# Gate and up projections as a 2x2 block product with seven products, the down projection in two passes, and weights split 1024 columns at a time

## The chip, the core and the metric

One Trainium2 chip, one of its cores. The metric is the device time of one execution in microseconds (us); lower is better. A core has a matrix engine (TensorE, in the profile PE, its weight loads PEld), a vector engine (VectorE, DVE), a scalar engine (ScalarE, ACT), a general engine (GpSimd, POOL) and queues that start transfers (SyncE, SP). Each engine takes its instructions in the order of its own list and waits for the others by semaphores.

## The reference

One transformer block on 512 tokens of width 1024 in float32: a norm, four token mixers (a forgetting attention, a short convolution, a chunkwise mLSTM, a sliding-window attention) with gated outputs, a merge product, and then the feed-forward part, which is where the change lies:

```python
h = rms_norm(x, ffn_norm[l])
act = jax.nn.silu(jnp.einsum('bsd,df->bsf', h, w_gate[l])) * jnp.einsum('bsd,df->bsf', h, w_up[l])
x = x + jnp.einsum('bsf,fd->bsd', act, w_down[l])      # D = 1024, D_FF = 2816 = 22 x 128
```

## The kernel before

Everything is held transposed: features on the 128 partitions, the 512 tokens along a row. A product of a 128 x 128 block of weights with 512 tokens is one matmul with the weights stationary. Precision comes from splitting: each float32 operand becomes a high part `hi` (a cast on ACT) and a remainder `lo` (`src - hi` on DVE), in `split` (L132); `mm3` (L127) then issues three matmuls, hi x hi, hi x lo and lo x hi, so every block product costs three.

All weights stream from one array of tiles of 1024 columns (512 KB). `w_load` (L151) starts a transfer on SP, `w_split` (L160) splits half a tile, 512 columns, into a pair of tiles from a ring of nine, and `w_take` (L174) hands out pairs some ahead of their use. `proj` (L394) makes one 128 x 512 output: eight input blocks, 24 matmuls.

The part around the change, in its order:

- Merge: eight outputs `mg` (L797). DVE adds the residual (`x`, L799), ACT and DVE scale and split it into `x2h`, `x2l` (L802), ACT squares it, and POOL adds the squares into `ssq` (L809) for the norm.
- 22 units, one for each 128 columns of the hidden layer (L814): `fg` (gate) and `fu` (up), 24 matmuls each, 48 in a unit. DVE multiplies both from PSUM by the norm's factor `r` (L820, L822), ACT applies Silu, POOL multiplies the two (L823), and the result is split into `ah`, `al`.
- Down: eight outputs `dn` (L831), each over all 22 units, 66 matmuls; DVE adds the residual and SP writes the block out.

Pools of fixed depth set when a buffer comes free: `wraw` for raw weight tiles, `whi`/`wlo` for split ones, eight PSUM banks in two pools (`mm`, `at`) of four. The program's instructions are put in order by a scheduler that works on a model of the times; the order that it gave is shown below where it matters.

## Time and profile before

| | us |
|---|---|
| Three runs | 863.06, 863.35, 864.82; median 863.35 |
| The profiled execution's own time | 862.88 |
| Its span in the trace | 861.1 |
| Mean granted clock of TensorE | 0.994 of full speed |
| Merge products, first to last start | 454.2 to 497.5 |
| Gate and up products, first to last start | 497.8 to 737.4 |
| Down products, first to last start | 737.6 to 857.1 |

The span is divided among stages that follow one another on PE. A busy PE is read with care, because matmuls overlap and their ends are modelled: the distance between the starts of two neighbours is what one costs. DVE, ACT and POOL rows have a real duration each; where a duration differs from the usual one for its shape, the instruction was held up while it ran. The idle time of an engine and its releaser say whom it waited for.

### The profile page before, as it was taken

How to read it: one execution, taken by the hardware profiler on the slowest of the kernel's cores; microseconds unless marked ns; L12 is line 12 of the kernel's file. 1: busy time of each engine (PE TensorE's matmuls, PEld its weight loads, DVE VectorE, ACT ScalarE, POOL GpSimd, SP SyncE). 2: the span in 40 equal slices, each digit the busy share in tenths (PEclk: the TensorE clock that was granted, in tenths of full speed). 3: DMA queues.
4: the chain of work that ended last, by engine and by line, in shares of the span. 5: the costliest groups of instructions: out<-in, count | busy, mean ns of one | idle time of the engine just before them, and what ended most of it. 6: DMA issues, size and time to landing. Idle time of an engine off the chain costs nothing.

```text
span 861.1 us, 10668 instructions
## 1 busy us (share of the span) xinstructions
PE 846.6 (98%) x3879; PEld 699.6 (81%) x3879; DVE 493.4 (57%) x899; ACT 386.1 (45%) x733; POOL 144.9 (17%) x134
## 2 busy tenths in 40 slices
PE   7999999999999999999999999999999999999998
PEld 6877788888788888888888888888888888888886
DVE  6899966459888886675745545444444333522320
ACT  7565555467665654554534444333333322322210
POOL 5262100024312001221211202111111111000000
PEclk9998999999999999999999999999999999999999
DMA  6642222242221522222224423222222232233310
GB/s 232 214 136 97 87 74 74 96 125 73 74 74 50 172 83 88 75 74 98 98 98 141 150 78 120 94 99 89 97 94 96 97 99 97 97 123 110 123 37 24
DMA packets 28520, 87.35 MB, mean 101 GB/s; under 512 B 3455, under 2 KB 5032, under 8 KB 28468
## 3 DMA queue, kind: packets, MB, share of 16 engines
q1 hardware_dynamic: 24716, 80.87, 27.6%
q10 hardware_dynamic: 3752, 5.81, 2.3%
q8 instruction: 30, 0.49, 0.2%
...
## 4 chain that ended last, share of the span: by engine, by line
PE 84%; DVE 8%; ACT 3%; issue 2%; DMA 2%; SPq 0%; POOL 0%; DVEq 0%; ACTq 0%; POOLq 0%
PE dn L130 5%; PE fu L128 5%; PE dn L129 5%; PE fg L128 5%; PE fu L130 5%; PE fg L130 5%; PE fu L129 5%; PE fg L129 5%; PE dn L128 5%; PE gswa L129 2%; PE gswa L128 2%; PE gswa L130 2%; PE gmlstm L128 2%; PE gmlstm L130 2%; PE mg L130 2%
## 5 line engine op out<-in xcount | busy, mean ns | idle before, releaser
L134 DVE TENSOR_TENSOR wl<-wr,wh 128x512 fp32r<-128x512 f32 x278 | 203.0, 733 | 154.9 <-ACT wh L133 153.6
L133 ACT CAST wh<-wr 128x512 fp32r<-128x512 f32 x278 | 170.4, 619 | 262.7 <-PE dn L129 69.1
L823 POOL TENSOR_TENSOR ut<-ut,gt 128x512 f32<-128x512 f32 x22 | 34.2, 1554 | 204.8 <-DVE ut L822 166.6
L129 PE MATMUL fu<-x2l,wh 128*128 128x512 f32 x176 | 68.5, 389 | 0.0
L128 PE MATMUL fu<-x2h,wh 128*128 128x512 f32 x176 | 68.5, 389 | 0.0
L130 PE MATMUL fg<-x2h,wl 128*128 128x512 f32 x176 | 68.5, 389 | 0.0
L130 PE MATMUL fu<-x2h,wl 128*128 128x512 f32 x176 | 68.5, 389 | 0.0
L128 PE MATMUL fg<-x2h,wh 128*128 128x512 f32 x176 | 68.5, 389 | 0.0
L129 PE MATMUL fg<-x2l,wh 128*128 128x512 f32 x176 | 68.5, 389 | 0.0
L128 PE MATMUL dn<-ah,wh 128*128 128x512 f32 x176 | 68.5, 389 | 0.0
L129 PE MATMUL dn<-al,wh 128*128 128x512 f32 x176 | 68.5, 389 | 0.0
L130 PE MATMUL dn<-ah,wl 128*128 128x512 f32 x176 | 68.5, 389 | 0.0
L130 PEld LDWEIGHTS fg<-x2h,wl 128*128 128x128 f32 x176 | 33.1, 188 | 6.9
L129 PEld LDWEIGHTS fu<-x2l,wh 128*128 128x128 f32 x176 | 33.1, 188 | 6.9
L128 PEld LDWEIGHTS dn<-ah,wh 128*128 128x128 f32 x176 | 33.0, 188 | 6.9
L129 PEld LDWEIGHTS dn<-al,wh 128*128 128x128 f32 x176 | 33.0, 188 | 6.9
L129 PEld LDWEIGHTS fg<-x2l,wh 128*128 128x128 f32 x176 | 33.0, 188 | 6.9
L128 PEld LDWEIGHTS fu<-x2h,wh 128*128 128x128 f32 x176 | 33.1, 188 | 6.8
L130 PEld LDWEIGHTS fu<-x2h,wl 128*128 128x128 f32 x176 | 33.0, 187 | 6.9
L130 PEld LDWEIGHTS dn<-ah,wl 128*128 128x128 f32 x176 | 33.0, 188 | 6.7
L128 PEld LDWEIGHTS fg<-x2h,wh 128*128 128x128 f32 x176 | 33.0, 188 | 6.7
L822 DVE TENSOR_TENSOR ut<-fu,r 128x512 f32<-128x512 f32 x22 | 15.2, 691 | 29.9 <-PE fu L130 29.9
...
## 6 DMA issues: line engine op xcount, KB each, us to landing
wr<-in_w_str_dram SPq DMA_DIRECT2D x139, 512.0 KB, 3.3
...
```

The source lines that it names most:

```text
L128: nc.tensor.matmul(out, a[0], b[0], start=start, stop=False)
L129: nc.tensor.matmul(out, a[0], b[1], start=False, stop=False)
L130: nc.tensor.matmul(out, a[1], b[0], start=False, stop=stop)
L133: nc.scalar.copy(hi, src)
L134: nc.vector.tensor_tensor(lo, src, hi.bitcast(F32), op=ALU.subtract)
L822: nc.vector.tensor_tensor(ut, pu, r2, op=ALU.mult)
L823: nc.gpsimd.tensor_tensor(ut, ut, gt, op=ALU.mult)
```

## The change

The gate and up projections of one unit are taken as one product of 2 x 2 blocks. On one side stands the input: four blocks, its feature halves (partition blocks 0 to 3 and 4 to 7) by its token halves (`t1`, `t2`, 256 tokens each). On the other stand the unit's weights: feature halves by gate and up. Seven block products replace eight (a Strassen-type scheme); each is four partition blocks by three matmuls of 256 columns, 84 matmuls in a unit. For that

- sums of input blocks are made once, on POOL, during the merge (`left_pair`), and split;
- sums of weight blocks are made for every unit on POOL (`ff_sums`: four subtractions of 512 columns) and split with the rest (`ff_split`: three tiles of 1024 columns and one of 512, for four of 512 before);
- the products are combined by six DVE operations of 256 columns that read PSUM and one copy on ACT (`unit`), and the multiplication by `r` moves in part to POOL, for down to the end of down;
- the merge outputs are made in the order 0, 4, 1, 5, 2, 6, 3, 7, and `r` is no longer applied to the up part but to the output of down.

Down is done in two passes, each over 11 units after those 11 are made, with the first pass added into the residual on POOL. Weights are split a whole tile of 1024 columns at a time (four tiles in each ring, four raw tiles for three before).

The diff, cut to its core:

```diff
-    "n_s": 58, "n_wk": 11, "w_raw": 3, "w_buf": 9, "w_ahead": 5, "mm": 4,
+    "n_s": 59, "n_wk": 11, "w_raw": 4, "w_buf": 4, "w_ahead": 4, "mm": 4,
...
     def w_split():
...
-        raw = stream["raws"][i // 2][:, (i % 2) * NT:(i % 2) * NT + NT]
-        hi = big.tile([P, NT], F32R, tag="whi", name=f"wh{i}", bufs=W_BUF)
-        lo = big.tile([P, NT], F32R, tag="wlo", name=f"wl{i}", bufs=W_BUF)
-        split(hi, lo, raw)
-        stream["ready"].append((hi, lo))
+        hi = big.tile([P, 2 * NT], F32R, tag="whi", name=f"wh{i}", bufs=W_BUF)
+        lo = big.tile([P, 2 * NT], F32R, tag="wlo", name=f"wl{i}", bufs=W_BUF)
+        split(hi, lo, stream["raws"][i])
+        for h in (slice(0, NT), slice(NT, 2 * NT)):
+            stream["ready"].append((hi[:, h], lo[:, h]))
...
+    def ff_sums(f):
...
+        r1, r2_ = ff_raw[f]
+        ta = big.tile([P, 2, NT], F32, tag="ysw", name=f"fta{f}", bufs=4)
+        t4 = big.tile([P, 2, NT], F32, tag="ysw", name=f"ftb{f}", bufs=4)
+        sub = lambda o, p, q: nc.gpsimd.tensor_tensor(o, p, q, op=ALU.subtract)
+        sub(ta[:, 0], r1[:, 1], r1[:, 0])
+        sub(ta[:, 1], r2_[:, 1], r1[:, 1])
+        sub(r1[:, 1], r2_[:, 1], ta[:, 0])
+        sub(t4[:, 0], r2_[:, 0], r1[:, 1])
+        ff_raw[f] = (r1, ta, r2_, t4[:, 0:1])
+
+    def ff_split(f, j):
...
+        src = ff_raw[f][j]
+        n = src.shape[1]
+        hi = big.tile([P, 2, NT], F32R, tag="whi", name=f"fh{f}_{j}", bufs=W_BUF)
+        lo = big.tile([P, 2, NT], F32R, tag="wlo", name=f"fl{f}_{j}", bufs=W_BUF)
+        split(hi[:, 0:n], lo[:, 0:n], src)
+        names = (("b11", "t2"), ("t1", "t3"), ("b21", "b22"), ("t4",))[j]
...
+    def left_pair(k):
+        lo_, hi_ = xg_f[k], xg_f[k + 4]
+        ss = [s_tile(f"ls{k}{i}") for i in range(2)]
+        sv = [ss[i // 2][:, (i % 2) * HT:(i % 2) * HT + HT] for i in range(4)]
+        t1, t2 = slice(0, HT), slice(HT, NT)
+        nc.gpsimd.tensor_tensor(sv[0], lo_[:, t2], hi_[:, t2], op=ALU.add)
+        nc.gpsimd.tensor_tensor(sv[1], sv[0], lo_[:, t1], op=ALU.subtract)
+        nc.gpsimd.tensor_tensor(sv[2], lo_[:, t1], lo_[:, t2], op=ALU.subtract)
+        nc.gpsimd.tensor_tensor(sv[3], hi_[:, t1], sv[1], op=ALU.subtract)
...
+        split(h[:, c], l[:, c], lo_[:, t1])
...
+        split(h, l, hi_)
...
+        for i in range(2):
+            h, l = s_tile(f"lh{k}{i}", F32R), s_tile(f"ll{k}{i}", F32R)
+            split(h, l, ss[i])
...
+    def product(ps, w, a, start, stop):
+        for k in range(4):
+            wb = slice(k * P, (k + 1) * P)
+            (wh, wl), (ah, al) = w, left[a][k]
+            nc.tensor.matmul(ps, wh[:, wb], ah, start=start and k == 0, stop=False, skip_group_check=True)
+            nc.tensor.matmul(ps, wh[:, wb], al, start=False, stop=False, skip_group_check=True)
+            nc.tensor.matmul(ps, wl[:, wb], ah, start=False, stop=stop and k == 3, skip_group_check=True)
...
+    def unit(f, ahead):
...
+        bA, bB, bC = ps_mm(f"fa{f}")[:, 0:HT], ps_at(f"fb{f}")[:, 0:HT], ps_mm(f"fc{f}")[:, 0:HT]
...
+        product(bA, op("b11"), "a11", True, True)
+        nc.scalar.copy(gt[:, t2], bA)
+        product(bB, op("t2"), "s2", True, True)
+        nc.vector.tensor_tensor(ut[:, t1], gt[:, t2], bB, op=ALU.add)
...
+        product(bC, op("t1"), "s1", True, True)
...
+        product(bB, op("t3"), "s3", False, True)
+        nc.vector.tensor_tensor(ut[:, t2], gt[:, t2], bB, op=ALU.add)
+        nc.vector.tensor_tensor(ut[:, t2], ut[:, t2], bC, op=ALU.add)
...
+        product(bA, op("b21"), "a12", False, True)
+        product(bB, op("t4"), "a22", False, True)
+        nc.vector.tensor_tensor(gt[:, t2], gt[:, t2], bB, op=ALU.add)
+        nc.gpsimd.tensor_tensor(gt[:, t2], gt[:, t2], r2[:, t2], op=ALU.mult)
+        nc.vector.tensor_tensor(gt[:, t1], bA, r2[:, t1], op=ALU.mult)
         nc.scalar.activation(gt, gt, AF.Silu)
+        product(bC, op("b22"), "s4", False, True)
+        nc.vector.tensor_tensor(ut[:, t1], ut[:, t1], bC, op=ALU.add)
...
+        nc.gpsimd.tensor_tensor(ut, ut, gt, op=ALU.mult)
         ah, al = s_tile(f"ah{f}", F32R), s_tile(f"al{f}", F32R)
         split(ah, al, ut)
...
+    for p in range(2):
+        act = []
+        for f in range(p * HB, p * HB + HB):
+            act.append(unit(f, next_unit(f + 1) if f + 1 < p * HB + HB else next_down(p)))
+        for d in range(KO):
+            ps = ps_mm(f"dn{p}_{d}")
...
+                nc.vector.tensor_tensor(o[:, c:c + n], ps[:, c:c + n], r2[:, c:c + n], op=ALU.mult)
+                if p == 0:
+                    nc.gpsimd.tensor_tensor(x2[d], x2[d], o, op=ALU.add)
+                else:
+                    nc.vector.tensor_tensor(o[:, c:c + n], o[:, c:c + n], x2[d][:, c:c + n], op=ALU.add)
+                    nc.sync.dma_start(outT[d * P:(d + 1) * P, c:c + n], o[:, c:c + n])
```

How the scheduler's order moves. First POOL, from the last accumulation of the merge gates to the feed-forward part. Before, between the accumulations `acc` and the first unit stand only the sums of squares:

```order
L731 TENSOR_TENSOR acc_1587<-acc_1587,tmlstm_4398 128x512
L731 TENSOR_TENSOR acc_1650<-acc_1650,tmlstm_4454 128x512
L731 TENSOR_TENSOR acc_1719<-acc_1719,tmlstm_4504 128x512
L809 TENSOR_TENSOR ssq_4512<-ssq_4512,x2sq_4600 128x512
L809 TENSOR_TENSOR ssq_4512<-ssq_4512,x2sq_4646 128x512
L809 TENSOR_TENSOR ssq_4512<-ssq_4512,x2sq_4692 128x512
L809 TENSOR_TENSOR ssq_4512<-ssq_4512,x2sq_4738 128x512
L809 TENSOR_TENSOR ssq_4512<-ssq_4512,x2sq_4784 128x512
L809 TENSOR_TENSOR ssq_4512<-ssq_4512,x2sq_4830 128x512
L809 TENSOR_TENSOR ssq_4512<-ssq_4512,x2sq_4876 128x512
L823 TENSOR_TENSOR ut_4967<-ut_4967,gt_4966 128x512
L823 TENSOR_TENSOR ut_5047<-ut_5047,gt_5046 128x512
```

In the changed program the same place reads as follows (`ls` are sums of input blocks; `fta`, `ftb` and a written `fr` are sums of weight blocks, here of the third unit; lines are those of the changed kernel):

```order
L884 TENSOR_TENSOR ssq_4230<-ssq_4230,x2sq_4504 128x512
L855 TENSOR_TENSOR ls_4507<-ls_4507,xgf_4460 128x256
L822 TENSOR_TENSOR fta_4796<-fs_4648,fr_4647 128x512
L857 TENSOR_TENSOR ls_4508<-xgf_4502,ls_4507 128x256
L822 TENSOR_TENSOR fr_4647<-fs_4648,fta_4796 128x512
L822 TENSOR_TENSOR ftb_4797<-fs_4648,fr_4647 128x512
L884 TENSOR_TENSOR ssq_4230<-ssq_4230,x2sq_4564 128x512
L854 TENSOR_TENSOR ls_4613<-xgf_4562,xgf_4608 128x256
L856 TENSOR_TENSOR ls_4614<-xgf_4562 128x256
L884 TENSOR_TENSOR ssq_4230<-ssq_4230,x2sq_4610 128x512
L855 TENSOR_TENSOR ls_4613<-ls_4613,xgf_4562 128x256
L857 TENSOR_TENSOR ls_4614<-xgf_4608,ls_4613 128x256
```

POOL's share of the merge grew from seven sums of squares to 35 rows: this piece, and 23 more between the last `acc` and its first row (16 input sums of 256 columns, 12 weight sums and seven sums of squares of 512). The weight sums of the first three units stand ahead of the last input sums (`ls_4613`, `ls_4614`), which need the last merge output.

Second DVE, in the middle of the units. Before, a unit (`ut_5127`, then the next, `ut_5207`) reads:

```order
L822 TENSOR_TENSOR ut_5127<-fu_5091,r_4879 128x512
L134 TENSOR_TENSOR wl_5191<-wr_5108,wh_5190 128x512
L134 TENSOR_TENSOR al_5133<-ut_5127,ah_5132 128x512
L134 TENSOR_TENSOR wl_5218<-wr_5108,wh_5217 128x512
L820 TENSOR_TENSOR gt_5206<-fg_5136,r_4879 128x512
L134 TENSOR_TENSOR wl_5236<-wr_5153,wh_5235 128x512
```

In the changed program, from a read of one unit's second half product to the next (`5564`/`5565` one unit, `5693`/`5694` the next, `fl` the `lo` tiles of the units behind them):

```order
L138 TENSOR_TENSOR fl_1_5633<-fta_5570,fh_1_5632 128x1024
L952 TENSOR_TENSOR ut_5694<-gt_5693,fb_5691 128x256
L138 TENSOR_TENSOR fl_2_5678<-fs_5438,fh_2_5677 128x1024
L963 TENSOR_TENSOR gt_5564<-gt_5564,fb_5562 128x256
L138 TENSOR_TENSOR fl_3_5682<-ftb_5571,fh_3_5681 128x512
L968 TENSOR_TENSOR ut_5565<-ut_5565,fc_5563 128x256
L138 TENSOR_TENSOR fl_0_5732<-fr_5566,fh_0_5731 128x1024
L958 TENSOR_TENSOR ut_5694<-gt_5693,fb_5691 128x256
L959 TENSOR_TENSOR ut_5694<-ut_5694,fc_5692 128x256
L138 TENSOR_TENSOR fl_1_5762<-fta_5699,fh_1_5761 128x1024
L965 TENSOR_TENSOR gt_5693<-fa_5690,r_4641 128x256
L138 TENSOR_TENSOR al_5687<-ut_5565,ah_5686 128x512
```

Splits of 1024 columns, which read SBUF twice, now alternate with short additions that read PSUM, and those of one unit stand behind splits that are for the next and the next but one.

## Rows read from the trace of the kernel before

**Rows 1.** Page, part 1: busy time, share of the span and instructions of each engine.

```profile
PE 846.6 (98%) x3879; PEld 699.6 (81%) x3879; DVE 493.4 (57%) x899; ACT 386.1 (45%) x733; POOL 144.9 (17%) x134
```

**Rows 2.** Windows: busy time and count by engine, granted clock, DMA share, GB/s.

```profile
0.00:455.00 455.00, 444.16 (x2105) 366.75 (x2106) 335.42 (x662) 258.71 (x527) 100.00 (x104) 0.99 0.31 104
455.00:498.00 43.00, 43.00 (x192) 35.59 (x191) 22.31 (x33) 18.70 (x31) 9.41 (x7) 1.00 0.46 145
498.00:617.00 119.00, 119.00 (x526) 98.53 (x525) 53.97 (x82) 45.77 (x73) 16.73 (x11) 1.00 0.28 97
617.00:737.60 120.60, 120.60 (x533) 99.85 (x532) 50.21 (x77) 39.93 (x66) 17.03 (x11) 1.00 0.29 96
737.60:858.00 120.40, 119.85 (x529) 98.91 (x527) 31.29 (x47) 22.97 (x37) 1.73 (x1) 1.00 0.25 86
```

**Rows 3.** Tile x2h: count, duration min/median/max, first and last start, forms.

```profile
L128 PEld LDWEIGHTS fg<-x2h,wh x176: 187/188/188, 497.5 to 731.3; 128*128 128x128 f32 x176
L128 PE MATMUL fg<-x2h,wh x176: 389/389/389, 497.8 to 731.5; 128*128 128x512 f32 x176
...
L130 PE MATMUL fu<-x2h,wl x176: 389/389/395, 503.9 to 737.4; 128*128 128x512 f32 x176
```

**Rows 4.** Timeline of PE at 256 columns: start, duration; every start between is equal.

```profile
275.78 0.28 PE L128 MATMUL pmv<-wh,xnh 128*128 128x256 f32 x1
...
279.74 0.28 PE L130 MATMUL pmv<-wh,xnl 128*128 128x256 f32 x1
```

**Rows 5.** Timeline of DVE, 207 to 210 us: start, duration.

```profile
207.38 0.69 DVE L730 SCALAR_TENSOR_TENSOR tfox<-tfox,ofox 128x512 f32<-128x512 f32 x1 [1.05 <-ACT tfox L725]
207.99 0.68 DVE L145 SCALAR_TENSOR_TENSOR sq2s<-sq2s,sq2v 128x512 f32<-128x512 f32 x1
208.59 1.78 DVE L134 TENSOR_TENSOR wl<-wr,wh 128x512 fp32r<-128x512 f32 x1
```

**Rows 6.** Timeline of POOL, the same stretch.

```profile
206.41 1.29 POOL L464 TENSOR_TENSOR sq1g<-sq1g,sq1s 128x512 f32<-128x512 f32 x1 [1.83 <-DVE sq1s L146]
208.15 1.67 POOL L731 TENSOR_TENSOR acc<-acc,tfox 128x512 f32<-128x512 f32 x1 [0.45 <-DVE tfox L730]
```

**Rows 7.** Groups of DVE, 498 to 737.6 us: busy, mean ns, idle before.

```profile
L820 DVE TENSOR_TENSOR gt<-fg,r 128x512 f32<-128x512 f32 x22 | 15.2, 691 | 21.6 <-PE fg L130 21.6
...
L134 DVE TENSOR_TENSOR al<-ut,ah 128x512 fp32r<-128x512 f32 x21 | 14.4, 692 | 27.6 <-ACT ah L133 27.5
```

**Rows 8.** Groups of DVE with 256 columns, whole span.

```profile
L134 DVE TENSOR_TENSOR ysl<-sw,ysh 128x256 fp32r<-128x256 f32 x8 | 3.4, 420 | 0.5 <-ACT ysh L133 0.5
...
L628 DVE TENSOR_TENSOR me<-ms,me 128x256 f32<-128x256 f32 x4 | 1.7, 425 | 0.9 <-POOL me L625 0.8
```

**Rows 9.** Groups of ACT, the cast at 512 and at 256 columns, whole span.

```profile
L133 ACT CAST wh<-wr 128x512 fp32r<-128x512 f32 x278 | 170.4, 619 | 262.7 <-PE dn L129 69.1 <-PE fu L129 64.4 <-issue 29.4
...
L133 ACT CAST ysh<-sw 128x256 fp32r<-128x256 f32 x8 | 3.3, 408 | 3.6 <-DVE sw L604 3.6
```

**Rows 10.** Group of POOL, 455 to 737.6 us, that met no other access.

```profile
L809 POOL TENSOR_TENSOR ssq<-ssq,x2sq 128x512 f32<-128x512 f32 x7 | 9.1, 1301 | 35.3 <-ACT x2sq L808 35.3
```

**Rows 11.** Tile xr: the additions behind the eight merge products.

```profile
L799 DVE TENSOR_TENSOR x<-mg,xr x8: 684/692/692, 463.1 to 498.0; 128x512 f32<-128x512 f32 x8
```

**Rows 12.** DMA issues: KB each, median us to landing.

```profile
wr<-in_w_str_dram SPq DMA_DIRECT2D x139, 512.0 KB, 3.3
```

**Rows 13.** Chain of waits, its end: start, duration.

```profile
857.49 0.42 DVE o L839
```

**Rows 14.** Windows of 3 us around a fall of TensorE's clock.

```profile
60.00:63.00 3.00, 2.04 (x6) 1.14 (x7) 2.90 (x4) 2.66 (x6) 1.08 (x1) 0.94 0.60 203
63.00:66.00 3.00, 3.00 (x11) 1.47 (x9) 2.94 (x4) 1.10 (x3) 0.00 (x0) 0.50 0.73 227
66.00:69.00 3.00, 3.00 (x7) 1.82 (x6) 2.94 (x5) 0.88 (x2) 1.28 (x1) 0.50 0.25 94
```

More of the change, by code (lines that the diff above doesn't have):

```diff
@@ L146, in rsqrt @@
         nc.vector.scalar_tensor_tensor(out, t, 1.5, y0, op0=ALU.add, op1=ALU.mult)
-    n_w = w_str.shape[0]
+    order = list(range(MG0)) + [MG0 + d for d in MG_ORDER]
+    n_w = len(order)
     stream = {"raw": 0, "split": 0, "raws": [], "ready": []}
@@ L156, in w_load @@
             raw = big.tile([P, 2 * NT], F32, tag="wraw", name=f"wr{i}", bufs=W_RAW)
-            nc.sync.dma_start(raw, w_str[i])
+            nc.sync.dma_start(raw, w_str[order[i]])
             stream["raws"].append(raw)
@@ L213, in flush @@
             bg()
-    warm = const.tile([P, NT], BF16, name="warm")
+    warm = s_tile("warm", BF16)
     nc.vector.memset(warm, 0.0)
@@ L789, with ff_load @@
     gated("mlstm", True)
-    x2, x2g = [], []
-    ssq2 = wk("ssq2")
-    for d in range(KO):
+    ff_raw, ff_op = {}, {}
+    def ff_load(f):
+        if f >= FB:
+            return
+        r1 = big.tile([P, 2, NT], F32, tag="wraw", name=f"fr{f}", bufs=W_RAW)
+        r2_ = big.tile([P, 2, NT], F32, tag="wraw", name=f"fs{f}", bufs=W_RAW)
+        src = w_str[FF0 + 2 * f:FF0 + 2 * f + 2]
+        nc.sync.dma_start(r1, src[:, :, 0:NT].rearrange("i p c -> p i c"))
+        nc.sync.dma_start(r2_, src[:, :, NT:].rearrange("i p c -> p i c"))
+        ff_raw[f] = (r1, r2_)
@@ L795 @@
+    for n, d in enumerate(MG_ORDER):
         xr = wk(f"xr{d}")
@@ L809 @@
             nc.gpsimd.tensor_tensor(ssq2, ssq2, sq, op=ALU.add)
-    r2 = s_tile("r2")
-    act = []
-    for f in range(FB):
-        pg = proj(f"fg{f}", x2g)
+        if n % 2:
+            left_pair(d - 4)
+        if n == 4:
+            ff_load(0)
+        if n == 5:
+            ff_sums(0)
+        if n == 6:
+            ff_load(1)
+            ff_split(0, 0)
+            ff_split(0, 1)
+        if n == 7:
+            ff_split(0, 2)
+            ff_split(0, 3)
+    r2 = s_tile("r2")
+    def product(ps, w, a, start, stop):
[5 more added lines that the diff above has]
+            nc.tensor.matmul(ps, wl[:, wb], ah, start=False, stop=stop and k == 3, skip_group_check=True)
@@ new lines, with dn_load @@
+    HB = FB // 2
+    CUT = ((0, 6), (6, 5))
+    dn = {"load": 0, "split": 0, "raw": {}, "op": {}}
+    dn_list = [(p, d, c) for p in range(2) for d in range(KO) for c in range(2)]
+    def dn_load():
+        i = dn["load"]
+        dn["load"] = i + 1
+        p, d, c = dn_list[i]
+        at, n = (d * FB + p * HB + CUT[c][0]) * P, CUT[c][1] * P
+        raw = big.tile([P, 2 * NT], F32, tag="wraw", name=f"dr{i}", bufs=W_RAW)
+        done = 0
+        while done < n:
+            t, o = divmod(at + done, 2 * NT)
+            m = min(n - done, 2 * NT - o)
+            nc.sync.dma_start(raw[:, done:done + m], w_str[DN0 + t, :, o:o + m])
+            done += m
+        dn["raw"][i] = raw
@@ new lines, in dn_split @@
+    def dn_split(to):
+        while dn["split"] < to:
+            i = dn["split"]
+            while dn["load"] < min(to + 1, len(dn_list)):
+                dn_load()
+            dn["split"] = i + 1
+            n = CUT[dn_list[i][2]][1] * P
+            hi = big.tile([P, 2 * NT], F32R, tag="whi", name=f"dh{i}", bufs=W_BUF)
+            lo = big.tile([P, 2 * NT], F32R, tag="wlo", name=f"dl{i}", bufs=W_BUF)
+            split(hi[:, 0:n], lo[:, 0:n], dn["raw"].pop(i)[:, 0:n])
+            dn["op"][i] = (hi, lo)
```

108 lines of the change are left out of this document (77 added, 31 removed).

## The prediction

> **What bounds the kernel now.** I read the page's busy times first: PE is busy 98% of the span, POOL 17% [rows 1]. Busy time alone does not say that PE is at its rate, so next the windows by stage: from the merge on PE has no idle time, at full granted clock, while DVE is busy 43% of the gate and up stage and POOL 14% [rows 2]. Then the rate itself. Gate and up are 1056 matmuls of 512 columns, the first starting at 497.8 and the last at 737.4 [rows 3]: 239.6 us over 1055 steps is 0.227 us each, so a unit of 48 takes 10.89 us. This stage waits for nothing; it gets shorter only by less work on PE, and longer as soon as another engine needs more than 10.89 us a unit.
>
> **PE's part of the change.** A unit becomes 84 matmuls of 256 columns. The trace has such matmuls with a new stationary block each: between the starts at 275.78 and 279.74 lie 33 steps, 0.120 us each [rows 4]. So 84 x 0.120 = 10.08 us, 0.81 us less a unit, 17.7 us over 22 units. A matmul of half the columns costs 53% and not half, which is why one product in eight saves only 7.4%. Down keeps its 528 matmuls, and its windows have no idle time to win [rows 2].
>
> **DVE and POOL: the price that the diff does not show.** The two are not independent. At 207.38 a DVE operation that reads one operand from PSUM ran beside a POOL operation, each at its usual length (0.69 and 1.29). But `sq2s`, which reads two SBUF operands, started at 207.99 and ended at 208.67; POOL's `acc`, started at 208.15, took 1.67 and ended at 209.82, 1.15 after DVE's end; and the split `wl` started at 208.59 took 1.78 instead of 0.69 and ended at 210.37, 0.55 after POOL's end [rows 5, 6]. Whoever came second waited for the other to end. A sum of squares that met nobody takes 1.30 [rows 10]. So POOL's two-operand work and DVE's splits share one way into SBUF, and it is held by one at a time: 1.15 us for 512 columns of POOL, 0.55 for a 512-column split.
>
> The Trainium skill says this too: GPSIMD Engine Reference, section 1 (Specifications), has the SBUF interfaces shared with VectorE, with contention when a DVE instruction has two SBUF inputs. The trace agrees, and it has the price that the page lacks; a reader who gives POOL its subtractions as free work beside DVE would get a stage at PE's 10.08 us.
>
> Now one unit's account of that shared way:
> - POOL: four weight subtractions and the product `ut` at 1.15, and the `gt` product of 256 columns at about half, 0.58: 6.33.
> - DVE: a split of 1024 columns is 0.55 plus 512 columns at the slope between 420 ns (256 columns) and 692 (512) [rows 7, 8], so 0.55 + 0.54 = 1.09; three of them, and two of 0.55 (`fl_3`, `al`): 4.37.
> - Together 10.70 us. Before, it was one POOL product and five splits, 1.15 + 2.75 = 3.90.
>
> The six PSUM additions of a unit (425 ns each alone [rows 8]) can run while POOL holds the way, so they add nothing if the queues alternate well. Thus even perfect alternation gives 10.70 and not 10.08 a unit, 4.2 us less than before over 22. It will not be perfect, for three reasons that the order shows. POOL waits in line between its `gt` and `ut` products for Silu on ACT (0.62 or more by the cast of that size [rows 9]) with the next unit's subtractions behind it. DVE's additions wait for PE's products with the next splits behind them. And the rings are four tiles deep: `fl_2` of a unit can be made only when the seventh product of the unit before has read its tile. From there the order on DVE is `fl_2`, an addition, `fl_3`, an addition, `fl_0` of the unit after: a cast of 1.04 (620 ns and 0.83 ns a column more [rows 9]), then 1.09 + 0.34 + 0.55 + 0.34 + 1.09 = 4.45 us, against three products (4.32) that PE has meanwhile. Each of the three splits can find POOL ahead of it, up to 1.15. With none, two units take 20.16 + 0.13; with all three, 23.7; since POOL holds the way more than half the time I take about 2 us, 22.2 for two units, 11.1 each: the shared way then carries 96% load. So waits cost 22 x (11.1 - 10.08) = 22.4 us against the 17.7 saved. Ends for a unit: 10.1 (no waits) and 11.9.
>
> Three units of each pass start with their weight sums made, during the merge or the first down pass; I give these six units half the waits: -3.1.
>
> ACT rises to about 5.4 us a unit (three casts of 1.04, three operations of 0.62, a copy of 0.4) and hides under PE. Loads keep their 1 MB a unit; one lands in 3.3 us [rows 12] and a raw tile is free about a unit early: nothing, and up to +5 if half rows land slower. In the down passes DVE gains a multiplication and, in the first, POOL an addition for each output of some 7.5 us, and SP some loads in two pieces; with DVE busy 31 of 120 us there before [rows 2] I cost this at nothing, and at 1.3 for each of the eight if POOL's additions met the splits at the worst moment.
>
> **From the merge to the first unit.** Before, each merge output needs one scaled split, and the last addition `x` ends at 498.7 [rows 11]; PE covers it. Now POOL has 35 operations in its list between the merge gates and the last input sums: 19 of 1.30 and 16 of about 0.72 (half, and the 0.15 by which 1.30 exceeds 1.15), 36 us alone. They can start when the second output is there: 463.1 and one pitch (498.0 - 463.1)/7 = 5.0, or some less since the first two end close together: about 467. That gives 503; the chain after the last `x` (scaling 0.7, four sums and a sum of squares 4.2, a split 1.2) gives 504.8. PE can go on with 42 matmuls that need no last sum, 5.0 us from 497.8: until 502.8. So at least 2 us are lost. If DVE's 17 us of splits in that stretch (five weight tiles, sixteen input splits, the first unit's weights) fell wholly on POOL, the sums would end near 518, a loss of 15. I take 6, nearer the lower end because much of DVE's work falls where POOL waits for data.
>
> **The rest.** At the end a second operation follows the last product: +0.4 by the 0.42 of the one there now [rows 13]. Splitting 1024 columns at a time in the first 455 us saves about 0.1 us of DVE per tile, and makes an urgent operation wait up to 0.5 longer behind one; PE has 11 us of idle there [rows 2], so -3 to +5; I take 0.
>
> **Sum** against the profiled execution's 862.9, which is 0.5 under the median: 862.9 - 17.7 + 22.4 - 3.1 + 6 + 0.4 = 870.9. I predict 871 us.
>
> **Rivals.**
> - *PE sets the pace.* DVE and POOL fit between one another, waits fall to 0.1 us a unit and the hand-over costs 2: 862.9 - 17.7 + 2.2 + 2 + 0.4 = 849.8. For it: PSUM additions stand between nearly all splits in the new order, room for POOL; products of the next unit stand between those of one, cover for PE. Against it: 10.70 is over 10.08 before any wait. It decides if the hold is shorter back to back than the pairs of the trace show.
> - *Waits and the clock.* At 60 to 63 us PE was busy 2.04 of 3 us, and from there the granted clock was 0.50 for some 6 us, 1.2 GHz, before it rose [rows 14]. If each pair of units has one such gap of 2 us and falls likewise, half of 6 us of products is lost each time, 11 x 3 = 33; PE's slowness lets the others catch up, so a third is regained: +22, 893. Against it: waits broken into short ones, as at 11.1, may leave the clock. The Trainium skill, TensorE: Matmul & The Clock Gate (HAM oscillation), also warns that idle gaps re-throttle the clock; here the rows show one and the rest of the trace does not settle when.
> - *Break even*: alternation near perfect, 862.9 - 4.2 + 2 + 0.4 = 861, and a microsecond or two of waits: 861 to 865.
> - *The halves don't come at 0.120*, since a weight load has a length of 0.19 of its own [rows 3]: 1848 x 0.19 = 351, near 974. The 33 equal steps with a load each [rows 4] speak against it.
>
> **Chances.** The forecast 0.45, PE's pace 0.30, the clock 0.15, break even 0.08, loads 0.02. What a measurement of this kernel can tell from no change is 0.2%, 1.7 us. Faster: 0.30 and 0.03 of break even; same 0.05; slower 0.62. The range reaches from just under PE's pace, 849, past the clock's, to 897. The forecast's own range is 864 to 882 (10.8 to 11.4 a unit, 2 to 10 at the hand-over).
>
> **What would show it.** After: PE starts 0.120 apart inside a product, with a gap once or twice in two units where it waits for a `fl` tile; two units 22.2 us apart; DVE's 1024-column splits with a mean well over 1.2 us and POOL's 512-column products over 1.3, because they hold each other; POOL busy over 70% in this stage; a gap of several us after the merge, released by a split of the last `ls`. Wrong it would be if POOL and DVE rows keep their lengths, if the units are 10.1 apart, or if the granted clock leaves 1.00 in the units.

## The result, and the profile after

The changed kernel takes 891.4 us (median of four runs, 889.35 to 893.29) against 863.4 before (863.06 to 864.82): ratio 1.032, 95% interval 1.029 to 1.035. It is slower by 28 us; the forecast was 871, 7.6 slower, in a range up to 897. The profiled run has 893.29 against 862.9, so 30.4 us are to be found.

The page's busy times, in the form of [rows 1]:

```profile
PE 844.9 (95%) x4671; PEld 732.5 (82%) x4671; DVE 605.9 (68%) x924; ACT 414.9 (47%) x683; POOL 361.5 (41%) x268
```

PE now has idle time, and POOL more than twice its work. The windows by stage, as in [rows 2]: the merge, the first unit, the other units of the first pass, its down, the units of the second pass, and below them two pieces of the first unit.

```profile
457.70:501.20 43.50, 43.50 (x193) 36.05 (x192) 25.01 (x23) 18.12 (x28) 30.07 (x22) 1.00 0.38 117
501.20:530.60 29.40, 17.23 (x87) 14.58 (x86) 16.96 (x21) 14.00 (x22) 16.93 (x16) 0.71 0.20 61
530.60:641.00 110.40, 103.22 (x820) 101.56 (x818) 90.00 (x112) 54.02 (x74) 86.11 (x52) 0.97 0.28 89
641.00:703.00 62.00, 62.00 (x287) 51.81 (x286) 26.25 (x30) 15.21 (x19) 24.88 (x17) 1.00 0.33 105
703.00:820.00 117.00, 109.02 (x878) 106.17 (x877) 95.72 (x112) 50.72 (x69) 95.34 (x57) 1.00 0.28 88
...
503.00:509.00 6.00, 2.03 (x13) 1.66 (x13) 4.32 (x5) 3.08 (x6) 5.08 (x5) 1.00 0.43 132
512.00:527.00 15.00, 9.11 (x34) 7.71 (x35) 7.87 (x11) 5.94 (x11) 7.51 (x8) 0.50 0.07 17
```

The merge starts at 457.7 instead of 454.2 and loses nothing itself. The first unit takes 29.4 us instead of some 10. The down pass has no idle time. The unit windows look harmless, PE busy 93%; the missing 7% is made of short breaks. In the second half of the second pass they come in the same four places of every second unit. PE's timeline, the longest of three such units and all four of the middle one:

```profile
756.14 0.39 PE L908 MATMUL fa<-a11h,fl 128*128 128x256 f32 x1 [1.24 <-DVE fl L138]
...
773.92 0.39 PE L908 MATMUL fa<-a2h,fl 128*128 128x256 f32 x1 [0.43 <-DVE fl L138]
775.95 0.39 PE L906 MATMUL fb<-lh,fh 128*128 128x256 f32 x1 [0.58 <-DVE ut L952]
777.80 0.39 PE L906 MATMUL fa<-a11h,fh 128*128 128x256 f32 x1 [0.17 <-ACT fh L137]
779.78 0.39 PE L908 MATMUL fa<-a11h,fl 128*128 128x256 f32 x1 [1.23 <-DVE fl L138]
...
803.44 0.39 PE L908 MATMUL fa<-a11h,fl 128*128 128x256 f32 x1 [1.24 <-DVE fl L138]
```

There two units are 23.65 us apart, where the forecast had 22.2. Counting PE's 256-column matmuls, 84 to a unit, shows that one unit of a pair takes 10.1 and the other 13.5. This holds for three pairs only. In the first pass the units behind the first take 10.1 to 13.7 in no fixed order, and over all 21 the waits are 24.5 us, 1.17 a unit (below).

Some of that is the clock. Behind the two longest breaks of PE in the units the granted clock is 0.50, 1.2 GHz:

```profile
564.55 0.39 PE L906 MATMUL fb<-a2h,fh 128*128 128x256 f32 x1 [2.08 <-DVE ut L958]
626.45 0.39 PE L906 MATMUL fa<-a2h,fh 128*128 128x256 f32 x1 [1.91 <-ACT gt L950]
```

```profile
565.48:568.89 3.41, 3.41 (x18) 3.41 (x17) 3.41 (x5) 0.62 (x1) 3.41 (x2) 0.50 0.00 0
626.92:630.33 3.41, 3.41 (x19) 3.41 (x18) 2.16 (x3) 1.04 (x2) 0.58 (x1) 0.50 0.11 27
```

The matmuls start 0.21 apart there instead of 0.12, which makes 2.9 of the 24.5 us.

I use four numbers for every kernel below: where the merge starts (before: 454.2); how long the first 84 matmuls take, from the start of the first to that of the last ("first unit"; PE needs 10.08); what the other 21 units and the down passes take over PE's 341.7 (22 x 10.08 + 119.9 for down) less the first unit's excess ("other waits"); and the tail. For the change, between its first unit's start at 501.23 and the last down product at 886.74:

| step | forecast | measured |
|---|---|---|
| PE's own work | -17.7 | -17.6 |
| other waits | 22.4 - 3.1 = 19.3 | 24.5 |
| hand-over: first unit over 10.08 | 6 | 19.3 |
| before the merge | 0 | 3.5 |
| tail | 0.4 | 0.7 |
| sum | 8.0 | 30.4 |

Where the other waits come from stands in the groups by operation for 710 to 820 us (columns as in [rows 7]), here of POOL, then of DVE, then of ACT:

```profile
L822 POOL TENSOR_TENSOR fr<-fs,fta 128x512 f32<-128x512 f32 x9 | 18.6, 2062 | 0.7
L822 POOL TENSOR_TENSOR fta<-fr 128x512 f32<-128x512 f32 x8 | 18.2, 2278 | 0.0
...
L964 POOL TENSOR_TENSOR gt<-gt,r 128x256 f32<-128x256 f32 x10 | 14.4, 1442 | 2.4 <-DVE gt L963 2.4
```

```profile
L138 DVE TENSOR_TENSOR fl<-fs,fh 128x1024 fp32r<-128x1024 f32 x10 | 18.5, 1846 | 1.0 <-ACT fh L137 1.0
...
L138 DVE TENSOR_TENSOR al<-ut,ah 128x512 fp32r<-128x512 f32 x9 | 13.6, 1509 | 0.0
```

```profile
L137 ACT CAST fh<-fr 128x1024 fp32r<-128x1024 f32 x9 | 9.4, 1045 | 11.6 <-POOL fr L822 10.8 <-PE fc L907 0.8
...
L966 ACT ACTIVATE gt<-gt 128x512 f32<-128x512 f32 x9 | 5.7, 632 | 28.1 <-POOL gt L964 28.1
```

POOL's 512-column operations have means of up to 2.28 (two groups are shown, the others have 1.31 to 1.72) where one alone has 1.30 [rows 10]; DVE's `al` has 1.51 where it had 0.69 [rows 7]. That was forecast. ACT's row was not: it stands idle for 28.1 us of 110 before Silu, until POOL's small product `gt` is done, and the casts of the next weights stand behind Silu.

### The profile page after: what moved, and what is told of

Its sections match the earlier page's. It is cut to its first block, busy times and chain, and to the rows that moved or that the text cites. A ratio compares the mean times of both kernels' runs of the same rounds, so it can differ in the third digit from the quotient of the medians.

```text
span 891.5 us, 12276 instructions
## 1 busy us (share of the span) xinstructions
PE 844.9 (95%) x4671; PEld 732.5 (82%) x4671; DVE 605.9 (68%) x924; ACT 414.9 (47%) x683; POOL 361.5 (41%) x268
## 4 chain that ended last, share of the span: by engine, by line
PE 57%; POOL 19%; DVE 9%; issue 5%; ACT 5%; DMA 5%; SPq 0%; DVEq 0%; ACTq 0%; POOLq 0%
POOL fta L822 6%; PE dn L132 4%; PE dn L133 4%; PE dn L134 4%; POOL fr L822 3%; DMA fs<-in_w_str_dram 3%; DVE fl L138 2%; POOL ftb L822 2%; POOL gt L964 2%; PE gswa L132 2%; PE gswa L133 2%; PE gswa L134 2%; PE gmlstm L132 2%; PE gmlstm L133 2%; PE gmlstm L134 2%
## 5 line engine op out<-in xcount | busy, mean ns | idle before, releaser
L138 DVE TENSOR_TENSOR wl<-wr,wh 128x1024 fp32r<-128x1024 f32 x73 | 98.3, 1347 | 35.5 <-ACT wh L137 34.9
L137 ACT CAST wh<-wr 128x1024 fp32r<-128x1024 f32 x73 | 76.4, 1047 | 55.7 <-issue 8.8
L133 PE MATMUL dn<-al,dh 128*128 128x512 f32 x176 | 68.5, 389 | 0.0
L134 PE MATMUL dn<-ah,dl 128*128 128x512 f32 x176 | 68.5, 389 | 0.0
L132 PE MATMUL dn<-ah,dh 128*128 128x512 f32 x176 | 68.4, 389 | 0.0
L906 PE MATMUL fb<-lh,fh 128*128 128x256 f32 x176 | 51.7, 294 | 5.1 <-ACT lh L137 3.3
L907 PE MATMUL fb<-ll,fh 128*128 128x256 f32 x176 | 50.9, 290 | 0.7 <-DVE ll L138 0.7
L908 PE MATMUL fb<-lh,fl 128*128 128x256 f32 x176 | 50.7, 288 | 0.0
L906 PE MATMUL fc<-lh,fh 128*128 128x256 f32 x176 | 50.4, 287 | 0.0
L907 PE MATMUL fc<-ll,fh 128*128 128x256 f32 x176 | 50.4, 287 | 0.0
```

What stands on the lines that cost most here:

```text
L132: nc.tensor.matmul(out, a[0], b[0], start=start, stop=False)
L133: nc.tensor.matmul(out, a[0], b[1], start=False, stop=False)
L134: nc.tensor.matmul(out, a[1], b[0], start=False, stop=stop)
L137: nc.scalar.copy(hi, src)
L138: nc.vector.tensor_tensor(lo, src, hi.bitcast(F32), op=ALU.subtract)
L906: nc.tensor.matmul(ps, wh[:, wb], ah, start=start and k == 0, stop=False, skip_group_check=True)
```

## The experiments

In the table, the ratio is to the kernel before, with its 95% interval; times after the ratio are from one profile each.

| kernel | us | ratio | merge starts | first unit | other waits |
|---|---|---|---|---|---|
| the change | 891.4 | 1.032 (1.029 to 1.035) | 457.7 | 29.4 | 24.5 |
| e1 no weight sums | 858.5 | 0.995 (0.993 to 0.998) | 458.5 | 20.3 | 0.4 |
| e2 five raw tiles | 885.9 | 1.026 (1.025 to 1.028) | 454.7 | 26.4 | 22.5 |
| e3 weight sums on DVE | 866.9 | 1.005 (1.003 to 1.006) | 458.3 | 24.3 | 4.5 |
| e4 input sums on DVE | 883.8 | 1.024 (1.023 to 1.026) | 454.7 | 23.6 | 23.7 |
| e5 both on DVE | 862.3 | 0.999 (0.998 to 1.000) | 457.2 | 19.8 | 4.8 |
| e6 and x rows earlier | 860.5 | 0.997 (0.995 to 0.998) | 456.7 | 17.9 | 4.4 |
| e7 unread subtractions | 881.3 | 1.021 (1.019 to 1.023) | 455.5 | 20.0 | 23.4 |
| e8 only x rows earlier | 886.2 | 1.026 (1.025 to 1.028) | 455.4 | 22.7 | 26.4 |
| e9 before, wide splits | 866.2 | 1.003 (1.002 to 1.005) | 459.0 | | |
| e10 before, subtractions | 863.7 | 1.001 (1.000 to 1.002) | 454.0 | | |
| e11 e7, `gt` on DVE | 868.0 | 1.006 (1.005 to 1.008) | 456.2 | 19.9 | 10.1 |
| e12 e6, two units on POOL | 863.1 | 1.000 (0.999 to 1.001) | 455.5 | 19.3 | 5.8 |
| e13 change, `gt` on DVE | 878.0 | 1.018 (1.016 to 1.019) | 456.5 | 27.2 | 12.5 |
| e14 e6, half splits | 859.2 | 0.996 (0.995 to 0.997) | 459.5 | 16.0 | 4.4 |
| e15 e11, `ut` on DVE too | 867.7 | 1.005 (1.004 to 1.007) | 458.6 | 20.3 | 9.8 |
| e16 e13, `ut` on DVE too | 877.5 | 1.016 (1.014 to 1.018) | 457.2 | 29.2 | 9.9 |

**The weight sums' price (e1), and where they are made (e3).**

```diff
-        sub(ta[:, 0], r1[:, 1], r1[:, 0])
...
-        ff_raw[f] = (r1, ta, r2_, t4[:, 0:1])
+        ff_raw[f] = (r1, r1, r2_, r2_[:, 0:1])
```

> The four weight subtractions of each unit are left out: the blocks as loaded are split in their place, so the output is another one. Theory A (POOL's two-operand work and DVE's splits share one way into SBUF): without the subtractions DVE's 1024-column splits fall from 1.6 to 1.8 us to about 1.2, the units come 10.1 to 10.2 us apart instead of 10.1 and 13.5 in turn, and the first unit after the merge, 29.4 us now, takes 15 to 20: 893.3 - 21 - 12 = about 860. Rival B (four raw tiles are too few: a load waits for a split, and the load, three sums, the cast and the split come one after the other) also gives 10.1 here, since the three sums leave that loop. Rival C (PE waits for its accumulators in PSUM, or for the additions that read them): units stay above 11 us, 875 or more.

```diff
-        sub = lambda o, p, q: nc.gpsimd.tensor_tensor(o, p, q, op=ALU.subtract)
+        sub = lambda o, p, q: nc.vector.tensor_tensor(o, p, q, op=ALU.subtract)
```

> The four weight subtractions of each unit on VectorE instead of GpSimd; nothing is left out. Theory A: a subtraction holds the shared way for 0.55 instead of 1.15 us, DVE's own work in a unit is 10.35 us (three splits of 1.23, two of 0.69, six additions of 0.42, four subtractions of 0.69), the units come 10.4 to 11.0 apart and the first unit takes some 8 us less: 893.3 - 21 x 0.7 - 8 = about 870. Rival D (DVE, in order, is the bound as soon as it has the sums too): 11.3 or more a unit, at 885 to 900.

Without the sums the other waits are gone (0.4) and the units come 10.1 apart: PE's part of the forecast holds, and rival C falls; A and B both expected this. On DVE the same sums leave 4.5 of 24.5, and the first unit loses 5 us. The total, 866.9, is a little under the 870 expected, and rival D (885 or more) falls.

**The raw ring (e2).**

```diff
-    "n_s": 59, "n_wk": 11, "w_raw": 4,
+    "n_s": 59, "n_wk": 9, "w_raw": 5,
```

> Five raw weight tiles in place of four; the 4 KB come from the ring of work tiles, nine in place of eleven. Rival B: the wait of POOL's second subtraction for the load (16.7 us in all) goes, two units take 21.2 us (POOL's 20.4 of work and 0.74 of wait) in place of 23.7, and the total is about 893.3 - 10 x 2.4 = 868. Theory A: POOL is busy 20.4 of 23.7 with lengthened operations and DVE's splits stay long; two units stay at 23 to 24 and the total within 4 us of the change's 891. Fewer work tiles may lengthen the first unit after the merge by some us in both.

The other waits fall by 2.0, not by 24: POOL's wait for the load, long as it is in the page, was not what ended last. Rival B falls, but the total, 885.9, is 5.5 us under the change's, more than the 4 allowed for. Between the two profiled runs lie 8.1 us: 3.0 are the start of the merge, which moves from profile to profile, and 3.0 the first unit.

**The hand-over (e4, e8, e5, e6, e12).** The chain that makes the last addition of the merge late can be followed in the change's timeline. Rows picked from the timelines of POOL, ACT and DVE, in order of time, from the sums of the third pair to the splits of the last:

```profile
508.52 1.27 POOL L822 TENSOR_TENSOR fta<-fs,fr 128x512 f32<-128x512 f32 x1
509.74 1.18 POOL L857 TENSOR_TENSOR ls<-xgf,ls 128x256 f32<-128x256 f32 x1
510.96 0.62 ACT L137 CAST lh<-ls 128x512 fp32r<-128x512 f32 x1 [1.84 <-POOL ls L857]
511.61 1.09 DVE L138 TENSOR_TENSOR ll<-ls,lh 128x512 fp32r<-128x512 f32 x1 [1.27 <-ACT lh L137]
512.62 0.68 DVE L875 TENSOR_TENSOR x<-mg,xr 128x512 f32<-128x512 f32 x1
513.33 0.72 ACT L878 ACTIVATE xgf<-x,col 128x512 f32<-128x512 f32 x1 [1.76 <-DVE x L875]
513.34 0.33 ACTq L872 DMA_DIRECT2D xr<-in_xT_dram  x1
516.12 0.68 DVE L875 TENSOR_TENSOR x<-mg,xr 128x512 f32<-128x512 f32 x1
518.31 0.73 POOL L856 TENSOR_TENSOR ls<-xgf 128x256 f32<-128x256 f32 x1
521.49 0.72 POOL L857 TENSOR_TENSOR ls<-xgf,ls 128x256 f32<-128x256 f32 x1
522.09 1.49 DVE L138 TENSOR_TENSOR ll<-ls,lh 128x512 fp32r<-128x512 f32 x2 [2.50 <-ACT lh L137]
522.24 0.62 ACT L137 CAST lh<-ls 128x512 fp32r<-128x512 f32 x1 [0.18 <-POOL ls L857]
```

PE had ended its last merge product before 502. The last two additions `x` come 11 and 15 us later, because the one stands in DVE's list behind a split that waits for POOL's sums of the pair before, and the other's load stands in ACT's list behind the scaling of the first.

```diff
-        nc.gpsimd.tensor_tensor(sv[0], lo_[:, t2], hi_[:, t2], op=ALU.add)
+        nc.vector.tensor_tensor(sv[0], lo_[:, t2], hi_[:, t2], op=ALU.add)
...
```

> Only the sixteen input sums at the merge go to VectorE; the weight subtractions stay on GpSimd. If the first unit's 29.4 us come from POOL's list, where the input sums stand between weight subtractions (POOL is busy without a break from 472 to 514), it falls to about 20 and with it the time at half clock (17 us now): 893.3 - 10 = about 883. If it is the shared way alone, whoever does the work, 27 to 30 and 891. The units' pitch stays at 23.7 for two in both cases.

For e8 and e6, with `xr_load()` called twice ahead of the loop and once at the head of each turn:

```diff
-        xr = wk(f"xr{d}")
-        nc.scalar.dma_start(xr, xT[d * P:(d + 1) * P, :])
+        xr_load()
+        xr = xrs[n]
```

> The change as it is, with the loads of the x rows at the merge issued two outputs earlier and nothing else. If the place of these loads in ACT's list makes the hand-over long, the first unit falls from 29.4 to 24 or less and the total to about 886. If it is POOL's list (the input sums behind weight subtractions), the first unit stays at 27 to 30 and the total at 889 to 893.

The edits of e3 and e4 together are e5:

> Weight subtractions and input sums both on VectorE; GpSimd keeps the sums of squares and the two products of a unit. Theory A (the shared way) with C (POOL's list at the merge): the first unit, 24.3 with the weight sums moved and 23.6 with the input sums moved, falls below the 20.3 that leaving the weight sums out gave, to about 18; units as with the weight sums moved, 10.1 to 11; total 866.9 - 6 = about 861. Rival D (DVE's list takes the place of POOL's: sixteen sums of 0.42 and twelve of 0.69 or more stand in order between its additions and splits): first unit 24 again, 867.

> The kernel with all sums on VectorE, and the loads of the x rows at the merge issued two outputs earlier on ACT's queue. If the last additions at the merge are late because each row's load stands in ACT's list behind the scaling of the output before (issue to landing 2.7 us, the last addition waits for it), the first unit gets 3 to 6 us shorter than with all sums on VectorE alone, about 857 in all. If DVE's own list holds the additions back, the same as without it, within 1 us.

Of the 19.3 us, e4 takes away 5.8, e8 6.6, e3 5.1; none alone is the cause. That is 17.5 added up, but together (e6) they take away 11.5 and leave 7.8: what they take away overlaps. The two combined kernels gained less than expected, e5 862.3 for 861, and e6 1.9 us of the first unit for 3 to 6, 860.5 for 857. Even without weight sums 10.2 remain (e1). In e6 a row of DVE suggested the next culprit, a sum for the second unit that waits for its load ahead of the last `x`:

```profile
503.23 1.18 DVE L822 TENSOR_TENSOR fta<-fs,fr 128x512 f32<-128x512 f32 x1 [2.08 <-DMA fs<-in_w_str_dram]
504.33 0.41 DVE L138 TENSOR_TENSOR a11l<-xgf,a11h 128x256 fp32r<-128x256 f32 x1
504.67 0.68 DVE L885 TENSOR_TENSOR x<-mg,xr 128x512 f32<-128x512 f32 x1
```

```diff
+        eng = nc.gpsimd if f in (1, 2) else nc.vector
-        sub = lambda o, p, q: nc.vector.tensor_tensor(o, p, q, op=ALU.subtract)
+        sub = lambda o, p, q: eng.tensor_tensor(o, p, q, op=ALU.subtract)
```

> All sums on VectorE and the x rows loaded earlier, but the weight sums of the second and third unit on GpSimd. In the kernel without this, DVE's last addition of the merge stands in order behind a subtraction that waits 2.1 us for a weight load. If that is what is left at the hand-over, the first unit falls from 17.9 to about 15 and the total from 860.5 to about 857.5. If POOL's subtractions then hold DVE's input sums (1.15 each, eight of them), the first unit stays at 17 to 20 and the total at 860 to 862.

The first of the two expectations was wrong, the second held but for 1 us: the first unit gets longer, 19.3, and the total is 863.1. Eight subtractions on POOL cost more than the wait.

Part of the hand-over is the clock. PE was busy 2.03 of the 6 us from 503 to 509, still at full clock, and from 512 to 527 the granted clock is 0.50, 1.2 GHz (windows above). The matmuls of the change's first unit show it, at the low and then at the full level:

```profile
518.98 0.41 PE L908 MATMUL fa<-a2h,fl 128*128 128x256 f32 x1
519.19 0.41 PE L906 MATMUL fa<-a2h,fh 128*128 128x256 f32 x1
...
529.49 0.28 PE L908 MATMUL fb<-lh,fl 128*128 128x256 f32 x1
529.61 0.28 PE L906 MATMUL fb<-lh,fh 128*128 128x256 f32 x1
```

Of the steps at 0.21 instead of 0.12 there are 26: some 2.5 us of the 19.3. The rest is waiting.

**The shared way, or only a long list (e7, e11, e13, e15, e16, e10).** e3 moved the sums and so changed two things, the load of the way into SBUF and POOL's list. In e7 the subtractions are made but nobody reads them:

```diff
+            for o in (ta[:, 0], ta[:, 1], t4[:, 0], t4[:, 1]):
+                nc.gpsimd.tensor_tensor(o, ff_raw["ut"], r2, op=ALU.subtract)
```

> The weight sums stay out of the products (the blocks as loaded are split, the output is another one), but GpSimd makes four subtractions of 512 columns a unit for all but the first two units, from tiles long ready (r2 and the last unit's product), into tiles that nobody reads. Theory A (shared way): POOL's operations take 1.7 to 2.0 in place of 1.3 and DVE's 1024-column splits 1.5 to 1.8, and the units are 10.7 or more apart though nobody waits for the subtractions: 858.5 + 18 x 0.6 to 1.2 = 869 to 880. Rival E (it is the length of the chain load, sums, cast, split, and not the way into SBUF): operations may get longer, but the units stay 10.1 to 10.2 apart, 858 to 861.

All but 1.1 of the other waits are back (23.4), though no product needs these sums; the total, 881.3, is even over the 869 to 880 expected. Groups of POOL and DVE in e7, 710 to 820 us:

```profile
L825 POOL TENSOR_TENSOR ftb<-ut,r 128x512 f32<-128x512 f32 x18 | 36.6, 2053 | 0.0
```

```profile
L138 DVE TENSOR_TENSOR al<-ut,ah 128x512 fp32r<-128x512 f32 x10 | 15.0, 1500 | 0.0
...
L963 DVE TENSOR_TENSOR gt<-fa,r 128x256 f32<-128x256 f32 x10 | 4.1, 411 | 0.0
```

The chain of load, sums, cast and split (rival E) is thus not the cause. But POOL's product `gt` still stood behind the subtractions; e11 takes it out of POOL's list, and e13 does the same to the change itself:

```diff
-        nc.gpsimd.tensor_tensor(gt[:, t2], gt[:, t2], r2[:, t2], op=ALU.mult)
+        nc.vector.tensor_tensor(gt[:, t2], gt[:, t2], r2[:, t2], op=ALU.mult)
```

> The kernel with the unread subtractions (weight sums left out of the products, the output another one), and the 256-column product with r2 moved from GpSimd to VectorE, so that ACT's Silu and the casts behind it no longer wait in line for POOL's list. Theory A (the way into SBUF): POOL still holds it 5 x 1.15 and DVE 4.37 + 0.3 of a unit, 10.4: the units stay at 10.5 or more on the mean and the total at 870 to 880. Rival F (POOL's list alone: its product stands behind subtractions, and ACT, in order, waits for it): the units fall to 10.1 to 10.3 and the total to 859 to 863.

> The change as it is, with the 256-column product with r2 on VectorE instead of GpSimd; the weight subtractions stay on GpSimd. If the unread subtractions' split holds here too (13.3 of 22.7 us from GpSimd's list, 9.5 from the way into SBUF), two units fall from 23.7 to 21.3 to 22.3 and the total from 891 to about 879. If in the change the subtractions are themselves waited for (by the casts of the sums), the list is as long as before less one product, and little is won: two units at 23 or more, 886 to 891.

The other waits fall from 23.4 to 10.1 in e7's program, and from 24.5 to 12.5 in the change's: one operation of 256 columns, on another engine, is worth 13 us of the 28. With the longest waits the falls of the clock in the units go too: they made 3.6 of e7's 23.4 and 2.9 of the change's 24.5, and there are none in e11 and e13. e13's total is what was expected; e11's, 868.0, lies between its two theories, so both hold in part. ACT's Silu in e13, with its wait:

```profile
L966 ACT ACTIVATE gt<-gt 128x512 f32<-128x512 f32 x11 | 7.0, 632 | 11.1 <-DVE gt L964 11.1
```

But ACT's cast `ah` now waits longer for POOL's other product, in e11:

```profile
L137 ACT CAST ah<-ut 128x512 fp32r<-128x512 f32 x10 | 6.2, 622 | 17.6 <-POOL ut L968 17.6
```

So e15 and e16 take that product out of POOL's list as well, from e11 and from e13:

```diff
-        nc.gpsimd.tensor_tensor(ut, ut, gt, op=ALU.mult)
+        nc.vector.tensor_tensor(ut, ut, gt, op=ALU.mult)
```

> The kernel with the unread subtractions (weight sums left out of the products, the output another one), with both products of a unit on VectorE: GpSimd has nothing in the units that any engine reads. If the way into SBUF alone makes waits, some 5 to 10 us of the other waits stay (account 4 x 1.15 + 4.37 + 0.3 + 0.55 = 9.8 of 10.08 us) and the total is 862 to 868. If it is GpSimd's list, waited for by ACT, they go: at most 2 us, 858 to 860.

> The change as it is, with both products of a unit on VectorE; GpSimd keeps the weight subtractions and the sums at the merge. If GpSimd's list is what is left, the other waits fall from 12.5 (one product moved) to below 6 and the total from 878 to about 871. If it is the way into SBUF, they stay at 10 or more and the total at 875 to 879.

In e15 POOL does nothing in the units that anybody waits for, and 9.8 us of waits stay. Its groups of DVE and what PE waits for from 527 us on (us in total, times, longest) tell by what:

```profile
L138 DVE TENSOR_TENSOR fl<-fs,fh 128x1024 fp32r<-128x1024 f32 x9 | 19.0, 2112 | 0.4 <-ACT fh L137 0.3
```

```profile
PE fa L906 <- DVE fl L138: 5.2, 7, 0.8
PE fa L904 <- ACT fh L137: 1.1, 1, 1.1
```

So the way alone, through lengthened splits, makes some 10 us in e15. DVE's own list, two products longer there, is not a likely cause: e3 puts four sums into it and leaves 4.5. In the change itself, taking `gt` out of POOL's list is worth 12.0 of the 24.5, taking out `ut` 2.6 more, and 9.9 are left (e16). These are not pure prices of the list. By the account the two moves also take 0.3 and 0.6 us a unit off the way, and 2.9 of the 12.0 are the clock. Nor are the 9.9 the way alone, since in e16 ACT's casts still wait for POOL's sums, here from 710 to 820 us:

```profile
L137 ACT CAST fh<-fr 128x1024 fp32r<-128x1024 f32 x8 | 8.4, 1047 | 10.2 <-POOL fr L822 10.2
```

e10 asks the same of the kernel before, whose account was 3.90 of 10.89 us a unit: the subtractions bring it to 8.5.

```diff
         nc.gpsimd.tensor_tensor(ut, ut, gt, op=ALU.mult)
+        for o in (ta[:, 0], ta[:, 1], t4[:, 0], t4[:, 1]):
+            nc.gpsimd.tensor_tensor(o, ut, r2, op=ALU.subtract)
```

> The kernel before with four subtractions of 512 columns on GpSimd in every gate and up unit, into tiles that nobody reads (nothing of the computation changes). By the account of the shared way a unit then holds it for 3.90 + 4 x 1.15 = 8.5 of its 10.89 us, so POOL's and DVE's operations get longer but the weight tiles split ahead still cover PE: the units stay at 10.89 and the total at 862 to 866. If POOL's work delays PE by itself, whatever the load of the way, as in the change, units of 11.5 to 12 and 877 or more.

Groups of DVE there, 500 to 737 us, first the kernel before and then e10:

```profile
L134 DVE TENSOR_TENSOR wl<-wr,wh 128x512 fp32r<-128x512 f32 x87 | 60.5, 695 | 54.1 <-ACT wh L133 54.1
```

```profile
L134 DVE TENSOR_TENSOR wl<-wr,wh 128x512 fp32r<-128x512 f32 x86 | 94.9, 1104 | 33.9 <-ACT wh L133 33.6
```

And POOL in e10, against [rows 10]:

```profile
L827 POOL TENSOR_TENSOR ftb<-ut,r 128x512 f32<-128x512 f32 x42 | 70.0, 1686 | 0.0
```

The splits grow from 695 to 1104 ns, and the units stay at 10.9 with 863.7 in all. Longer operations alone cost nothing here, with an account well under PE's time.

The Trainium skill says in SBUF — State Buffer, section "SBUF: two separate sides", that the pair of ports which GpSimd shares with VectorE is locked by whichever operation starts first, for the whole instruction, and that the other blocks. e7 and e10 agree with it: both engines' operations get longer, while DVE's operation with an operand from PSUM keeps its 0.41 (e7's `gt<-fa,r`).

The Trainium skill's page Perfetto Trace Analysis (Optimizing Scalar/DVE Operations) warns that moving operations between those two engines might not help because of this port. Here it does: e3 against the change, 1.005 against 1.032. A subtraction has 0.68 on DVE in three of e3's four groups (0.92 in the other) and 1.54 to 2.28 on POOL in the change; how much of the gain is this and how much POOL's shorter list, e3 does not separate.

**Before the merge (e9, e14).** In e9 the split of a whole raw tile is one operation, as in the change:

```diff
-        raw = stream["raws"][i // 2][:, (i % 2) * NT:(i % 2) * NT + NT]
-        hi = big.tile([P, NT], F32R, tag="whi", name=f"wh{i}", bufs=W_BUF)
...
+        hi = big.tile([P, 2 * NT], F32R, tag="whi", name=f"wh{i}", bufs=W_BUF)
```

> The kernel before with one edit of the change: weights split 1024 columns at a time (four raw tiles, four pairs of split tiles). If that edit makes the part before the merge 2 to 3.5 us longer (in the profiles of the change and its variants the merge starts at 454.7 to 458.5, before it was 454.2): 865 to 867. If those differences come from the clock, which falls at other places from one execution to the next: 861 to 864.5, no difference to be told.

e9 is 3.1 us slower than the kernel before (1.0034, 1.0022 to 1.0046), so the edit costs time, and the change's 3.5 us are of that size. The rival, the clock, is not excluded by this. Up to 440 us the change and e4 run the same list of operations on DVE, ACT and POOL, and e4's merge starts at 454.7. Of the 3.0 us between the two, 0.9 are there by 14 us, 1.5 come with a fall of the clock at 26.2 and 0.5 with one at 227.6; e4's profile has neither. Windows of the change, then of e4, then of e9, whose merge starts at 459.0:

```profile
20.00:30.00 10.00, 8.37 (x38) 7.33 (x38) 8.97 (x10) 2.55 (x6) 4.95 (x4) 0.83 0.60 175
```

```profile
20.00:30.00 10.00, 9.31 (x50) 8.09 (x49) 8.08 (x10) 1.75 (x5) 4.14 (x3) 1.00 0.55 184
```

```profile
20.00:30.00 10.00, 8.36 (x35) 7.50 (x35) 8.98 (x10) 2.56 (x6) 4.96 (x4) 0.75 0.58 187
```

Without any fall before the merge, e4 starts it 0.7 us after e10 (454.0), which has none either. The profile before has falls too, at 21.7 and 62.6, and starts the merge at 454.2. Whether the edit brings the falls, or only makes them cost more, stays open. In e14 each tile is split in two halves again:

```diff
+        h = slice((i % 2) * NT, (i % 2) * NT + NT)
+        hi, lo = (t[:, h] for t in stream["hl"])
+        split(hi, lo, stream["raws"][i // 2][:, h])
```

> All sums on VectorE, the x rows loaded earlier, and the weights of the part before the merge split 512 columns at a time again, two halves of one tile; loads, rings and everything after the merge stay. If the width of the splits costs the 3 us before the merge, the merge starts at about 454 instead of 456 to 458 and the total falls from 860.5 to about 857.5. If it is the rings (four raw tiles, four pairs of 1024 columns) or the joined tiles, the total stays at 860 to 861.

The median is 1.4 us lower than e6's, but the intervals overlap, and its merge starts at 459.5 in the profile, which has the clock at 0.50 from 24.5 to 31.3: the width is not shown to be the cause. Whether it is the shorter rings or the joined tiles of the first weights stays open.

e6 and e14 compute all of it and beat both kernels, the one before by 0.3 and 0.4%.

## Why the prediction was right in direction and too small

- *PE's part*: right. Steps of 0.120, units of 10.1 wherever nothing waits, -17.6 for -17.7 (22 x 0.81 is 17.8).
- *The shared way*: right as a mechanism. DVE's and POOL's lengthened rows were forecast, e7 makes the waits with subtractions that nobody reads, e10 shows the account under which they cost nothing. That the stage would not run at PE's pace (the 0.30 rival) was right too; e1 gives that pace only without the sums.
- *The wait per unit, mis-sized*: the step that took "about 2 us, 22.2 for two units", of bounds of 20.16 and 23.7. Three pairs of the second pass have 23.65, the upper bound; over all units the waits are 24.5 for 19.3. (The 0.34 for an addition in these bounds has no row: [rows 8] have 0.42, which raises both by some 0.2.) Two sentences in it failed. "ACT ... hides under PE": by busy time it does, but in order it stands at Silu for POOL's product, 28.1 us of 110, with the casts behind. And the `gt` product at "about half, 0.58": it takes 1.44 there and stands behind lengthened subtractions. I named POOL's wait for Silu and not Silu's wait for POOL. Taking `gt` out of POOL's list is worth 12 of the 24.5 us (e13), the clock's share of 2.9 and the shorter account included. The account does not give the waits by itself: with both products moved it is 9.8, under PE's 10.08, and 9.9 us of waits are left (e16).
- *The hand-over, mis-sized most*: "I take 6, nearer the lower end because much of DVE's work falls where POOL waits for data". Measured 19.3, over even the upper end of 15, and the largest part of the miss: 13.3 of 22.4 us. The premise did not hold: from 472, when it can start, to 514 POOL waits only 2.6 us. Its 35 rows take 44.7 us for the 36 costed alone, 8.7 of the 17 that the bound allowed for DVE's splits, and with 5.2 us of waits in all the last sum ends at 522.2, 21.0 after the unit's first product, where the upper bound (518, though 503 + 17 is 520) had 20.2. What the bound lacked are the loads of the x rows in ACT's list (e8: 6.6) and the fall of the clock (some 2.5), which I had only as a rival for the units.
- *Before the merge*: "-3 to +5; I take 0". It is +3.5. The edit costs 3.1 in e9; of the 3.0 us by which the change trails e4 there, 2.0 come with falls of the clock, which the term did not have. The gain of 0.1 us a tile does not show.
- *Loads and down*: about right as costed. A fifth raw tile takes 2 us off the waits; the down window has no idle time.
- *Waits and the clock*: 893 was near the measured 891 by luck. It had one fall of the clock in each pair of units, +22 us; the units have two in all, 2.9 us, and the long one is at the hand-over. By my own sign ("if the granted clock leaves 1.00 in the units") the forecast was wrong there, by this little. The measured time lies in my range only because I stretched it to this rival; the forecast's own 864 to 882 misses it.
